# Filler matmuls of a hybrid encoder's two attentions, listed by hand for three zones

## The chip, the cores and the metric

The kernel runs on one core of a Trainium2 chip. The core has TensorE (PE, matrix products into PSUM), VectorE (DVE), ScalarE (ACT), GpSimd (POOL) and SyncE (SP, which here only issues DMAs). The metric is the device time of one execution in microseconds; the time before is the median of three executions, 1702.64 us (1701.64 to 1703.32).

## The reference

Two layers of an encoder on one sequence of 512 tokens with 1024 features. Per layer:

```python
h = rms_norm(x, attn_norm_g[l])
c_q, c_kv, k_rope, gq, gk, gv, pool_in, gate_logits = split_columns(h @ w_in[l], IN_SIZES)
o_mla  = mla_branch(...)   # 8 heads; q = rms_norm(c_q) @ w_uq, k and v from rms_norm(c_kv) @ w_ukv,
                           # q and k of 96 (64 + 32 rotary) normalised per head
o_gqa  = gqa_branch(...)   # 8 heads of 64 on 2 key/value heads, normalised, rotary
o_pool = pool_branch(...)  # centred means over 2/4/8/16 tokens minus the token, mixed per group
gates  = sigmoid(gate_logits)                      # 3 x 1024 per token
merged = gates[0] * (o_mla @ w_branch_mla) + gates[1] * (o_gqa @ w_branch_gqa) \
       + gates[2] * (o_pool @ w_branch_pool)
x = x + merged @ w_out[l]
x = x + GatedMLP(rms_norm(x, ffn_norm_g[l]))       # width 2816, depthwise conv of 3
```

## The kernel before

Activations lie feature-major in SBUF (128 features by 512 tokens). For precision every operand of a product is split into a high and a low part, and each product is three matmuls (`mm3`: high by high, high by low, low by high). Weights come by DMA in a fixed order of pieces (`w_dma`, three raw buffers ahead), and ScalarE and GpSimd split each piece (`w_split`: `wh`, then `wl`).

The program is written out by hand-made scheduling at build time. `Clock` holds a planned time; `chain` queues the follow-up steps of a result on VectorE, ScalarE and GpSimd at the planned time at which they can run; `need` advances the planned time until a key is recorded by `done`; `has` asks whether a key has been recorded by now and says no for one that is not there. The order of the instructions on each engine comes from this plan; on the chip semaphores keep the data right.

A layer does, in order: latents and the pool branch; keys and values of the grouped attention; its queries; then three steps with two attentions in them:

- the first attention (`gqa`), then the second (`mla`), eight heads each. `attention` walks a list of steps with places (`PLAN`): transposes of the queries and keys (`t_q`, `t_k`, PSUM bank `mi`), four score products with a row maximum on VectorE (`s_max`, bank `S`, result `nm`), the maxima as a row (`m_row`, bank `mi`, written into `qa`), and for each of four key blocks the transposed scores (`probs`, two banks `ST`), exponential `pe`, high part `ph`, low part `pl`, and the value products (`av_hi` with `ph`, `av_lo` with `pl`, bank `AV`). `o_out` copies a head's output, takes the reciprocal of the sums and splits the product (`oh`, `ol`).
- between these steps PE is given other matmuls, the filler. Its units are three matmuls (six for the latent units): a gate block `g` has 8 units and a branch block `b` has 4, both 512 columns wide; `q` (4 units) and `n` (2) make half of the latent attention's queries and keys, `v` (2) half of its values. All use the two PSUM banks `acc`. `Filler.step` runs one unit, `upto` runs up to a count, `finish` the rest.
- before, the filler of the first attention is made of the pool branch's gates and blocks, both `q` and both `n`; that of the second of the grouped branch's gates and blocks and both `v`; the latent branch's gates and blocks run after it. `_order` lists them: a gate block, then the branch block before it, with the latent units put in at places given by `EXTRA`.

Ahead of the first attention the filler runs for 13 units and then until the keys and queries are recorded as ready; ahead of the second for 17 units and then in this loop:

```python
fb.upto(PRE_B)
while not ck.has(("mq", l, 0)) and fb.step():
    pass
attention("mla", fb, "om", omla)
```

`q_norm(g)`, the last of the queries' steps, ends with `done("mq", l, g)`; `t_q` of the second attention asks for `("mq", l, h // 4)`.

Of the kernel before, what the change touches and what calls it, by code (L numbers as in the profile page):

```python
# [18 lines left out]
P = 128  # L19
T = 512  # L20
# [9 lines left out]
NSLOT = 53  # L30
RAW = 3
EXTRA = (("q", 2, (2, 5)), ("n", 2, (6, 7)), ("v", 1, (0, 3)))
# [25 lines left out]
def _order(br):  # L58


    r = []
    for m in range(KC + 1):
        r += [(k, pos.index(m)) for k, b, pos in EXTRA if b == br and m in pos]
        if m < KC:
            r.append(("g", m))
        if m > 0:
            r.append(("b", m - 1))
    return r
# [6 lines left out]
def _widths():  # L75

    r = [384] * KC + [T] * 8 + [288] * KC + [T] * 4 + [T] + [T] * 4
    for br in (2, 1, 0):
        for k, _ in _order(br):
            r += WIDTHS[k]  # L80
    return r + [T] * (2 * KC) + [T] * (4 * FC) + [T] * (2 * FC)
# [162 lines left out]
def trunk(ctx: ExitStack, tc: tile.TileContext, x, w, prm, gb, cst, out):  # L244
# [244 lines left out]
    def layer(l, sq, xsrc):  # L489
# [289 lines left out]
        def gates(br, okey, odst, mode):  # L779
            hold = {}  # L780

            def gate(m):
                acc = ps("acc")
                yield from feat_major(acc, G1)
                t = hold[m] = slot("gt")

                def logits():
                    V.tensor_tensor(t[:, :T], acc, nrm["rbc"][:, :T], ALU.mult)
                    free("acc")

                chain(([("rbc", G1)], logits), lambda: A.activation(t[:, :T], t[:, :T], AF.Tanh, scale=0.5))

            def branch(m):
                acc = ps("acc")
                wh, wl = wnext()
                for kc in range(4):
                    if kc:
                        yield
                    need((okey, l, kc))
                    ws = slice(kc * P, kc * P + P)  # L800
                    oh, ol = odst[kc]
                    mm3(acc, wh[:, ws], wl[:, ws], oh[:, :T], ol[:, :T], kc == 0, kc == 3)
                t = hold.pop(m)

                def product():
                    dst = XM[:, m, :] if mode == "first" else t[:, :T]
                    V.scalar_tensor_tensor(dst, t[:, :T], 1.0, acc, ALU.add, ALU.mult)
                    free("acc")

                def add():  # L810
                    (V if mode == "last" else G).tensor_tensor(XM[:, m, :], XM[:, m, :], t[:, :T], ALU.add)

                def fin():
                    SY.dma_start(XM[:, m, :], xsrc[m])
                    done("mrg", l, m)

                if mode == "first":
                    chain(product)
                elif mode == "add":
                    chain(product, add)  # L820
                else:
                    mh, ml = slot("mgh", F32R), slot("mgl", F32R)
                    merged[m] = (mh, ml)
                    chain(product, add, *split(mh[:, :T], ml[:, :T], XM[:, m, :]), fin)

            extra = None
            for k, m in _order(br):
# [3 lines left out]
                work = branch(m) if k == "b" else gate(m)  # L831
                more = True
                while more:
                    if extra:
                        if next(extra, END) is END:
                            extra = None
                        yield
                    more = next(work, END) is not END
                    yield
# [4 lines left out]
        krr = small("krr", [P, 4, 32], bufs=1)  # L844

        def make_q(g):
# [53 lines left out]
        def make_n(g):  # L900
# [9 lines left out]
            if g == 0:  # L910
                return
            kj_ = small("kj", [P, 4, 32], bufs=1)
            kss = small("kss", [P, 4], bufs=1)

            def sums():
                V.tensor_reduce(kss, kj_, AX.X, ALU.add)
                for i in range(2):
                    V.tensor_tensor(ss[:, 1, i], ss[:, 1, i], bc(kss.unsqueeze(2), [P, 4, 4]), ALU.add)
                V.tensor_scalar(ss[:, 1], ss[:, 1], 1.0 / 96, EPS, ALU.mult, ALU.add)
# [4 lines left out]
            chain(*rope_steps(krr, krt, tabm[:, 256:384].rearrange("p (b f) -> p b f", b=4),  # L924
                              tabm[:, 384:512].rearrange("p (b f) -> p b f", b=4), [P, 4, 32], 16, V),
# [581 lines left out]
```

## Time and profile before

| | |
|---|---|
| median of three executions | 1702.64 us |
| the profiled execution | 1701.64 us |
| its span, first to last instruction | 1699.4 us |
| mean granted TensorE clock | 0.994 |
| PE busy | 1655.1 us, 97% |
| DVE, ACT, POOL busy | 938.3, 782.6, 972.3 us |
| first attention with its filler, layer 0 | about 113 to 245 us |
| second attention with its filler, layer 0 | about 245 to 373 us |
| gates and blocks behind it, layer 0 | about 373 to 441 us |

A row of the views below names line, engine, operation, output and inputs; in a window's row each engine has its busy time and count, and PEclk is the granted share of the TensorE clock. PE's busy times are modelled for pipelined matmuls, so that the starts of two neighbours say more than the length of one.

### The profile page before, as it was taken

Reading aid. Unit: us, or ns where it says so; the run is one execution under the profiler, and the core shown is the slowest. Engines: PE = TensorE matmul, PEld = TensorE weight load, DVE = VectorE, ACT = ScalarE, POOL = GpSimd, SP = SyncE. Lnnn points to the kernel's source line nnn. Section 1 sums busy time; section 2 is a strip of 40 time slices with the busy share of each in tenths; the row PEclk is TensorE's granted clock in tenths of the full one; section 3 lists DMA queues with packets and bytes.
Section 4 is the critical chain, followed back from the end, with each engine's and each line's share of the span. In section 5 each row is a group of like instructions: output and inputs, shape, how many; then the busy total and the mean of one; then the engine's idle time right before and its main releaser. Section 6 shows DMA issues by size and latency. Waiting matters only on the chain.

```text
span 1699.4 us, 20370 instructions
## 1 busy us (share of the span) xinstructions
PE 1655.1 (97%) x7360; PEld 1335.7 (79%) x7360; DVE 938.3 (55%) x1502; ACT 782.6 (46%) x1375; POOL 972.3 (57%) x771
## 2 busy tenths in 40 slices
PE   8889999999999999999999899999999999999999
PEld 7767767778888888888888677777788888888887
DVE  6765976643356666630156759766433666666100
ACT  5356655653344444433234576556534444444221
POOL 4455565764566566655545565666645665666543
PEclk9999999999999999999999999999999999999999
DMA  5221112113423332333333211111233232232331
GB/s 176 85 72 44 56 48 62 38 62 112 124 87 89 98 100 87 100 106 116 100 101 95 70 44 47 61 49 38 75 118 118 87 100 92 94 94 93 111 118 56
DMA packets 44596, 145.40 MB, mean 86 GB/s; under 512 B 5072, under 2 KB 6352, under 8 KB 44496
## 3 DMA queue, kind: packets, MB, share of 16 engines
q1 hardware_dynamic: 44352, 144.10, 27.0%
q8 instruction: 58, 0.95, 0.2%
q14 instruction: 42, 0.34, 0.1%
q10 hardware_dynamic: 144, 0.01, 0.0%
HBM read 139.90 MB, written 4.19 MB: 85 GB/s over the span
## 4 chain that ended last, share of the span: by engine, by line
PE 87%; DVE 8%; issue 2%; ACT 1%; POOL 1%; DMA 0%; SPq 0%; POOLq 0%; DVEq 0%; ACTq 0%
PE ps_acc L341 40%; PE ps_ST L341 23%; PE ps_AV L341 20%; PE ps_S L341 2%; DVE gqr L216 1%; PE ps_mi L345 1%; DVE yt L216 1%; DVE nm L224 1%; POOL wl L216 1%; PE ps_mi L341 1%; DVE MQ L216 1%; DVE yt L220 0%; DVE win L216 0%; DVE y L220 0%; DVE y L228 0%
## 5 line engine op out<-in xcount | busy, mean ns | idle before, releaser
L216 POOL TENSOR_TENSOR wl<-raw,wh 128x512 fp32r<-128x512 f32 (+1 forms) x514 | 678.5, 1330 | 493.4 <-ACT wh L209 432.1
L209 ACT ACTIVATE wh<-raw 128x512 fp32r<-128x512 f32 (+3 forms) x522 | 313.8, 608 | 194.2 <-PE ps_ST L341 70.8
L220 DVE SCALAR_TENSOR_TENSOR a<-u,prm,a 128x512 f32<-128x512 f32 x176 | 239.6, 1362 | 79.2 <-ACT a L209 74.0
L341 PE MATMUL ps_acc<-HH,wh 128*128 128x512 f32 x624 | 247.1, 396 | 2.2 <-DVE XM L220 2.2
L341 PE MATMUL ps_acc<-HH,wl 128*128 128x512 f32 x624 | 246.7, 395 | 1.2 <-POOL wl L216 1.2
L341 PE MATMUL ps_acc<-HL,wh 128*128 128x512 f32 x624 | 246.2, 395 | 0.0
L216 POOL TENSOR_TENSOR pl<-pe,ph 128x512 fp32r<-128x512 f32 x105 | 138.9, 1325 | 110.4 <-ACT ph L209 70.4
L341 PEld LDWEIGHTS ps_acc<-HH,wh 128*128 128x128 f32 x624 | 117.5, 188 | 30.8 <-ACT mns L209 2.1
L341 PEld LDWEIGHTS ps_acc<-HH,wl 128*128 128x128 f32 x624 | 117.3, 188 | 30.0 <-POOL wl L216 2.5
L341 PEld LDWEIGHTS ps_acc<-HL,wh 128*128 128x128 f32 x624 | 117.5, 188 | 26.8
L209 ACT ACTIVATE pe<-ps_ST 128x512 f32<-128x512 f32 x128 | 76.3, 596 | 101.8 <-PE ps_ST L341 100.4
L224 DVE TENSOR_REDUCE nm<-ps_S 128x1 fp32r<-128x512 f32 x128 | 87.8, 686 | 57.3 <-PE ps_S L341 57.0
L216 POOL TENSOR_TENSOR al<-a,ah 128x512 fp32r<-128x512 f32 x44 | 58.1, 1320 | 84.8 <-ACT ah L209 56.5
L341 PE MATMUL ps_AV<-HH,wh 128*128 128x512 f32 x256 | 101.3, 396 | 0.0
L341 PE MATMUL ps_AV<-HH,wl 128*128 128x512 f32 x256 | 101.2, 395 | 0.0
L341 PE MATMUL ps_AV<-HL,wh 128*128 128x512 f32 x256 | 101.1, 395 | 0.0
L341 PE MATMUL ps_ST<-HH,wh 128*128 128x512 f32 x240 | 95.0, 396 | 0.0
L341 PE MATMUL ps_ST<-HH,wl 128*128 128x512 f32 x240 | 94.8, 395 | 0.0
L341 PE MATMUL ps_ST<-HL,wh 128*128 128x512 f32 x240 | 94.8, 395 | 0.0
L209 ACT ACTIVATE a<-u,prm 128x512 f32<-128x512 f32 x88 | 71.8, 816 | 32.4 <-DVE u L216 32.4
L209 ACT ACTIVATE ah<-a 128x512 fp32r<-128x512 f32 x44 | 27.8, 632 | 116.2 <-DVE u L240 110.8
L209 ACT ACTIVATE a<-a 128x512 f32<-128x512 f32 x44 | 27.8, 633 | 113.5 <-DVE u L240 113.5
(332 smaller groups left out, 3563.3 us busy)
## 6 DMA issues: line engine op xcount, KB each, us to landing
raw<-w SPq DMA_DIRECT2D x229, 512.0 KB, 3.5
raw<-w SPq DMA_DIRECT2D x13, 384.0 KB, 3.0
XM<-x SPq DMA_DIRECT2D x16, 256.0 KB, 3.8
raw<-w SPq DMA_DIRECT2D x6, 448.0 KB, 3.4
xsp<-XM SPq DMA_DIRECT2D x8, 256.0 KB, 2.0
XM<-xsp SPq DMA_DIRECT2D x8, 256.0 KB, 3.2
out<-XM SPq DMA_DIRECT2D x8, 256.0 KB, 2.5
raw<-w SPq DMA_DIRECT2D x4, 432.0 KB, 3.2
```

Of the source, the lines that this page charges most:

```text
L209: return self.eng.activation(out, in_, func, **k)
L216: return self.eng.tensor_tensor(out, *a)
L220: return self.eng.scalar_tensor_tensor(out, *a)
L224: return self.eng.tensor_reduce(out, in_, *a, **k)
L341: PE.matmul(o, lhsT=lhsT, rhs=rhs, start=start, stop=stop)
L345: PE.transpose(o, src, ident)
```

## The change

The filler is no longer made per branch but listed for three zones: beside the first attention, beside the second, and behind it. Zone 0 loses the second `q` and `n` and gains three gate blocks of the grouped branch (126 units for 108). Zone 1 has the rest of that branch, both `v`, the second `q` and `n`, and three gate blocks of the latent branch (106 for 100). Zone 2 is what is left (72 for 96). The results of gates that run ahead are held in SBUF slots, of which there is one more. The normalisation of the latent queries and keys is made per half, with its own sums, reciprocal roots and ready keys, and the key's rotary part with the first `n`. The weight pieces are packed in the new order. The loop ahead of the second attention asks for another key.

```diff
-NSLOT = 53
+NSLOT = 54
-EXTRA = (("q", 2, (2, 5)), ("n", 2, (6, 7)), ("v", 1, (0, 3)))
+ZONES = (
+    "g20 g21 b20 q0 g22 b21 g23 b22 g24 b23 n0 g25 b24 g26 b25 g27 b26 g10 b27 g11 g12",
+    "v0 g13 g14 q1 b10 g15 n1 b11 g16 b12 v1 g17 b13 g00 b14 g01 b15 g02 b16 b17",
+    "g03 g04 g05 g06 g07 b00 b01 b02 b03 b04 b05 b06 b07")
...
+def _zone(z):
+    return [(k[0], int(k[1]) if len(k) == 3 else None, int(k[-1])) for k in ZONES[z].split()]
...
-            if g == 1:
-                chain(([("ssq", l, i, b) for i in range(2) for b in range(4)],
-                       lambda: V.tensor_scalar(ss[:, 0], ss[:, 0], 1.0 / 96, EPS, ALU.mult, ALU.add)),
-                      *rsqrt_steps(ss[:, 0].rearrange("p g b c -> p (g b c)"), 32, ("ssmq", l)),
-                      *[z for i in range(2) for z in q_norm(i)])
+            chain(([("ssq", l, g, b) for b in range(4)],
+                   lambda: V.tensor_scalar(ss[:, 0, g], ss[:, 0, g], 1.0 / 96, EPS, ALU.mult, ALU.add)),
+                  *rsqrt_steps(ss[:, 0, g].rearrange("p b c -> p (b c)"), 16, ("ssmq", l, g)), *q_norm(g))
...
-            chain(lambda: V.tensor_tensor(kj_, krt, krt, ALU.mult), ([("ssn", l, i, p) for i in range(2) for p in range(2)], sums),
-                  *rsqrt_steps(ss[:, 1].rearrange("p g b c -> p (g b c)"), 32, ("ssm", l)),
-                  *[z for i in range(2) for z in k_norm(i)])
+            chain(([("ssn", l, g, 0), ("ssn", l, g, 1), ("kss", l)], sums),
+                  *rsqrt_steps(ss[:, 1, g].rearrange("p b c -> p (b c)"), 16, ("ssm", l, g)), *k_norm(g))
...
-        fa = Filler(gates(2, "op", opool, "first"), units(2))
+        def filler(z):
+            return Filler(work(z), sum(UNITS[k] for k, _, _ in _zone(z)))
+        fa = filler(0)
...
-        fb = Filler(gates(1, "og", ogqa, "add"), units(1))
+        fb = filler(1)
         fb.upto(PRE_B)
-        while not ck.has(("mq", l, 0)) and fb.step():
+        while not ck.has(("mq", l, 0, 3)) and fb.step():
             pass
         attention("mla", fb, "om", omla)
-        Filler(gates(0, "om", omla, "last"), units(0)).finish()
+        filler(2).finish()
```

More of the change, by code (lines that the diff above doesn't have):

```diff
@@ L77, in _widths @@
     r = [384] * KC + [T] * 8 + [288] * KC + [T] * 4 + [T] + [T] * 4
-    for br in (2, 1, 0):
-        for k, _ in _order(br):
+    for z in range(3):
+        for k, _, _ in _zone(z):
             r += WIDTHS[k]
@@ L777, in layer @@
         merged = {}
[L779 to L824, printed above, removed]
@@ new lines, in layer, with gate, logits @@
+        ogqa, omla, hold = {}, {}, {}
+        branches = {2: ("op", opool, "first"), 1: ("og", ogqa, "add"), 0: ("om", omla, "last")}
+        def gate(br, m):
+            acc = ps("acc")
+            yield from feat_major(acc, G1)
+            t = hold[br, m] = slot("gt")
+            def logits():
+                V.tensor_tensor(t[:, :T], acc, nrm["rbc"][:, :T], ALU.mult)
+                free("acc")
+            chain(([("rbc", G1)], logits), lambda: A.activation(t[:, :T], t[:, :T], AF.Tanh, scale=0.5))
@@ L826, in gates, with work @@
+        def work(z):
             extra = None
-            for k, m in _order(br):
+            for k, br, m in _zone(z):
                 if k in mla_make:
@@ L830, in gates @@
                     continue
-                work = branch(m) if k == "b" else gate(m)
+                step = branch(br, m) if k == "b" else gate(br, m)
                 more = True
@@ L837, in gates @@
                         yield
-                    more = next(work, END) is not END
+                    more = next(step, END) is not END
                     yield
```

64 lines of the change are left out of this document (40 added, 24 removed).

## The prediction

> **What bounds the kernel now.** I read the page first, then the stretches, the waits of TensorE, and the timeline around the second attention.
>
> ```profile
> span 1699.4 us, 20370 instructions
> ...
> PE 1655.1 (97%) x7360; PEld 1335.7 (79%) x7360; DVE 938.3 (55%) x1502; ACT 782.6 (46%) x1375; POOL 972.3 (57%) x771
> ...
> PE 87%; DVE 8%; issue 2%; ACT 1%; POOL 1%; DMA 0%; SPq 0%; POOLq 0%; DVEq 0%; ACTq 0%
> ```
>
> TensorE (PE) is busy for 97% of the span and is 87% of the chain that ended last. So a change of order can win only PE's idle time, and it loses wherever it makes PE wait. The stretches of layer 0 show where that idle time is (first attention 113 to 245 us, second 245 to 373, the rest of the third gates 373 to 441):
>
> ```profile
> core 0: us, PE busy (x) PEld busy (x) DVE busy (x) ACT busy (x) POOL busy (x), PEclk, DMA share, GB/s
> 113.00:245.00 132.00, 121.60 (x538) 94.72 (x539) 102.28 (x164) 87.06 (x157) 71.78 (x58) 0.97 0.15 47
> 245.00:373.00 128.00, 127.86 (x597) 101.78 (x596) 77.38 (x114) 71.85 (x128) 83.49 (x75) 1.00 0.17 53
> 373.00:441.00 68.00, 68.00 (x294) 54.98 (x293) 25.45 (x37) 24.70 (x42) 32.73 (x27) 1.00 0.39 116
> ```
>
> The first attention leaves PE idle for 10.4 us, the second for 0.14 us, the last stretch for none. The second attention is thus already covered by the gate and branch matmuls mixed into it. What PE waits for in the first one:
>
> ```profile
> PE ps_S L341 <- DVE nm L224: 4.3, 4, 2.7
> PE ps_mi L345 <- DVE gk L216: 3.7, 1, 3.7
> PE ps_acc L341 <- ACT mqs L209: 1.2, 2, 0.9
> ...
> PE ps_acc L341 <- DVE vml L216: 0.9, 1, 0.9
> ```
>
> **The change, part by part.** The diff moves work, and it also changes one key. Before, the loop ahead of the second attention takes single units of filler until `("mq", l, 0)` is recorded; now it asks for `("mq", l, 0, 3)`. The only writer, at the end of `q_norm`, still records `("mq", l, g)`. The four-part key is never written, so the loop ends only when `fb.step()` has nothing left: all 106 units of the second zone go ahead of the attention, and the attention gets none. The order of the changed kernel's instructions on TensorE bears this out. After the last branch matmul come transposes, scores and values alone, up to the last head:
>
> ```
> L338 Matmult ps_acc_3052<-oh_2407,wl_3015 128x512
> L342 Matmult ps_mi_3071<-C,MQ_84 96x128 x4
> L342 Matmult ps_mi_3082<-C,MK_86 96x128 x4
> L338 Matmult ps_S_3093<-kh_3087,qa_3077 128x512
> L342 Matmult ps_mi_3096<-C,MQ_84 96x128 x4
> L338 Matmult ps_S_3103<-kh_3087,qa_3077 128x512
> ```
>
> So the main cost is a second attention without cover, twice. TensorE runs the same matmuls in all.
>
> *PE's work in the bare attention.* Matmuls of 512 columns start every 0.233 us, and a row of four transposes takes 0.35:
>
> ```profile
> 269.38 0.60 PE L345 MATMUL ps_mi<-C,MK 128*96 128x128 f32 x4
> 269.73 0.47 PE L341 MATMUL ps_ST<-qa,kl 96*128 96x512 f32 x1
> ...
> 360.79 0.39 PE L341 MATMUL ps_ST<-qa,kh 100*128 100x512 f32 x1
> 361.02 0.40 PE L341 MATMUL ps_AV<-ph,vmh 128*128 128x512 f32 x1
> ...
> 361.22 0.60 ACT L209 ACTIVATE pe<-ps_ST 128x512 f32<-128x512 f32 x1 [1.24 <-PE ps_ST L341]
> ...
> 361.85 0.63 ACT L209 ACTIVATE ph<-pe 128x512 fp32r<-128x512 f32 x1
> ...
> 362.56 1.29 POOL L216 TENSOR_TENSOR pl<-pe,ph 128x512 fp32r<-128x512 f32 x1 [0.90 <-ACT ph L209]
> ```
>
> A head has four score maxima (S), four key blocks of three probability matmuls (P) and three value matmuls (two with ph, one with pl), which is 28 x 0.233, and 0.70 for its transposes and 0.06 for the row of maxima (M): 7.28 us. Eight heads: 58.3 us.
>
> *The waits.* A block's chain starts with its third P: 0.43 to the exponential, 0.63, 0.71 and 1.29 to the end of pl, 0.1 to PE: 3.16 us. In the built order the pl matmul of block k stands ahead of P of block k+2, with only block k+1 between. Two blocks hence take at least 3.16 + 3 x 0.233 = 3.86, and a head 7.7. The side engines add their queues, with these durations:
>
> ```profile
> L224 DVE TENSOR_REDUCE nm<-ps_S 128x1 fp32r<-128x512 f32 x32 | 22.0, 686 | 13.5 <-PE ps_S L341 13.4
> L236 DVE RECIPROCAL osum<-osum 128x128 f32<-128x128 f32 x16 | 14.6, 930 | 0.0
> L220 DVE SCALAR_TENSOR_TENSOR qb<-ps_mi,gcol,qa 96x512 fp32r<-96x512 f32 x8 | 5.7, 716 | 5.6 <-ACT qa L209 5.6
> ...
> L216 DVE TENSOR_TENSOR qa<-ps_mi,C 4x512 fp32r<-4x512 f32 x8 | 5.5, 684 | 1.7 <-PE ps_mi L341 1.5
> L216 DVE TENSOR_TENSOR kl<-ps_mi,kh 96x512 fp32r<-96x512 f32 x8 | 5.5, 682 | 0.2
> ...
> L232 DVE CAST ph<-pe 128x512 fp32r<-128x512 f32 x8 | 4.8, 602 | 12.5 <-ACT pe L209 10.2 <-POOL XM L216 2.2
> ...
> 358.25 1.01 DVE L216 TENSOR_TENSOR oraw<-oraw,osum 128x512 f32<-128x512 f32 x1
> ...
> L209 ACT ACTIVATE qa<-ps_mi,gcol 96x512 fp32r<-96x512 f32 x8 | 5.4, 674 | 5.5 <-PE ps_mi L345 5.5
> L209 ACT ACTIVATE kh<-ps_mi 96x512 fp32r<-96x512 f32 x7 | 4.1, 590 | 0.0
> L209 ACT ACTIVATE oh<-oraw 128x512 fp32r<-128x512 f32 x4 | 2.5, 629 | 6.2 <-DVE oraw L216 6.2
> L216 POOL TENSOR_TENSOR ol<-oraw,oh 128x512 fp32r<-128x512 f32 x3 | 3.9, 1293 | 1.3 <-ACT oh L209 1.3
> L240 POOL MEMSET kh<- 4x512 f32 x8 | 4.5, 563 | 0.5
> ```
>
> I walk one head, zero at its first P, each engine in its built order. A plain head: P to 0.7, transposes of the next keys, kh to 2.0, kl to 2.7; transposes of the next queries after it (one bank, mi); S0 at 2.1 and its nm to 3.45; S1 at 3.7; pl of block 0 ready at 3.45; block 2 ends near 4.9; qb and nm1 put S2 at 5.6; block 3 follows pl of block 1 (6.3); S3 at 7.2, its nm to 8.3, M at 8.4, three value matmuls, next P at 9.1. A head beside which a pair's output is normalised has four reciprocals between the maxima: from nm0 at 2.97, VectorE runs 4 x 0.69 + 4 x 0.93 + 0.72 + 0.68 without a gap to 10.3, and the next head's third P needs its last result (the row of maxima): 9.8. In the head after it, oh stands ahead of the exponential (0.7 later) and ol with the memset ahead of pl (pl of block 0 ends near 5.0): 9.5. Ahead of head 0 the first transposes, qb, kl, four S and nm, and M follow each other with nothing beside: 9.1. The last head runs to its last pl: 9.5. Sum: 9.1 + 2 x 9.1 + 3 x 9.8 + 2 x 9.5 + 9.5 = 85.2 us, of which PE works 58.3. **Waits: 26.9 us per layer.** Lowest: 9.1 + 8 x 7.7 - 58.3 = 12.4. Highest: 36, if the side engines' operations collide (an oraw product took 1.01 us, a cast of ph took 0.60) and each head takes 1.1 more. I take the walk.
>
> *The clock.* After an idle stretch PE runs at half clock:
>
> ```profile
> 50.08:53.49 3.41, 1.39 (x6) 0.76 (x5) 3.41 (x8) 0.61 (x2) 0.98 (x1) 1.00 0.00 0
> 53.50:56.91 3.41, 1.13 (x3) 0.54 (x3) 3.38 (x16) 0.63 (x1) 0.00 (x0) 0.50 0.00 0
> ...
> 190.03:193.44 3.41, 3.41 (x9) 2.64 (x9) 3.38 (x7) 1.75 (x3) 0.28 (x1) 0.50 0.29 119
> 900.00:903.41 3.41, 1.95 (x13) 1.50 (x12) 3.41 (x5) 2.97 (x7) 1.82 (x3) 1.00 0.00 0
> ...
> 190.58 0.63 PE L341 MATMUL ps_acc<-opl,wh 128*128 128x512 f32 x1
> 191.00 0.63 PE L341 MATMUL ps_acc<-oph,wl 128*128 128x512 f32 x1
> ```
>
> At 190 us, after the wait of 2.7 us, matmuls start every 0.42 to 0.43 us for 3.41 us: some 8 of them, 0.195 later each, 1.6 us lost. The window with 1.39 us busy was followed by half clock, that with 1.95 was not. The bare attention's start holds 1.7 us of PE work in 9.1, so half clock follows it: **+1.6 per layer** (0 to 4).
>
> *First attention.* Its filler grows from 108 units to 126, and half of the latent queries' and keys' normalisation leaves its VectorE, busy for 102.28 of 132 us. The gk wait stays (it stands ahead of the moved work), as does the one on vml. Of the remaining 10.4 - 3.7 - 0.9 = 5.8 us, and the 1.6 of half clock behind the longest wait, I take two thirds: **-5.0** (0 to -7.4).
>
> *Ahead of the second attention.* q and n units now stand between branch units that hold the other of the two acc banks, so each waits for the last one's evacuation: **+1.0**, about what the same units cost in the first attention (ACT mqs 1.2); 0 to 4. The 42 further small VectorE operations are mostly the second copies of the reciprocal root's steps:
>
> ```profile
> L220 DVE SCALAR_TENSOR_TENSOR yt<-yt,y x36: 152/190/1190, 30.3 to 1334.5; 128x8 f32<-128x8 f32 x18, 128x32 f32<-128x32 f32 x12, 128x40 f32<-128x40 f32 x6
> ```
>
> At a median of 0.19 us the 21 of a layer are 4 us. They are hidden by VectorE's idle 50 us of 128; uncovered they would cost those 4 us. Weights are only reordered: same DMAs on SP's queue, same halves; ScalarE and POOL keep up, as with this mix in 373 to 441 us. The second attention's own idle 0.14 goes: **-0.1**. The last zone shrinks by 24 units that ran without idle time and run without it elsewhere: 0. The slot more only takes memory.
>
> Sum per layer: 26.9 + 1.6 - 5.0 + 1.0 - 0.1 = 24.4; two layers 48.8. The profiled execution took 1701.64 us (span 1699.4), 1.0 below the median of 1702.64, so against that median 1751.
>
> **Rivals.**
> *The clock stays low.* The walk's thinnest 3.41 us in a head with reciprocals holds some 1.6 us of matmul starts, 2.2 busy as the windows count, not far above 1.95. If every other window ran at half clock, PE's 7.28 us per head would take 3.1 more; with half of it on the path, 8 x 1.5 = 12 per layer: 1775. Against it: the one window of 1.95. The Trainium skill, "TensorE: Matmul & The Clock Gate", section "HAM oscillation — how this bites in real kernels", asks only for gaps under about 3.4 us, by which no wait between heads would lower the clock; the trace disagrees, as 2.7 us did. Its section on the second failure mode says that frequent small gaps make the clock swing; that would be this rival.
> *The side engines do better.* Without weight splits and gates, ACT and POOL are free when a block arrives, and a head takes 8.4, midway between the chain's 7.7 and the plain head's 9.1: waits 9.1 + 67.2 - 58.3 = 18.0, sum per layer 15.5, 1734. Against it: the order of VectorE's queue between the maxima is fixed.
> *Not slower: the change does what its words say.* If the loop ahead of the second attention stopped early, as before, the attention would keep its cover and only the first one's gain would stay: 2 x -5.0, 1693. It decides from some 35 units (three matmuls, 0.70 us each) left beside the attention, which cover those 24.4 us. Against it: the built order, where none is left.
>
> **How the numbers follow.** Forecast 1751: 0.60; clock stays low 0.16; side engines do better 0.19; not slower 0.05, most of it below. The forecast's neighbours reach down to the lowest waits with the full gain (2 x (12.4 + 1.6 - 7.4 + 1.0 - 0.1) = +15, 1718) and up to highest waits with half clock recurring (2 x (36 + 4 - 3 + 1) = +76, 1779, with the clock's 24 more 1803). The range 1725 to 1788 leaves out about 2 in 10. 0.2% (3.4 us) is about what a measurement can tell. Slower 0.95, within it 0.01, faster 0.04.
>
> **What would show it.** In the changed profile: in each layer some 85 us of second attention with PE busy near 70% and only scores, values and transposes on it; PE's waits led by pl from POOL, nm and the row qa from VectorE, and kl; half clock at the start of each; under 7 us idle in the first attention; no idle time in the last zone. A head period of 8.4 or less, filler between the heads, or half clock in most windows would make it wrong.

## The result, and the profile after

The changed kernel takes 1780.99 us (median of four executions, 1777.66 to 1783.73) against 1702.98 us for the kernel before in the same series: 1.0455 times as long, 95% interval 1.0429 to 1.0481. That is 78 us more, where the forecast had 48.8. The profiled execution has a span of 1781.9 us.

From here on a line number of the changed kernel is three lower than the same line's before (L341 is L338, L216 is L213). The page after, with the rows that the prediction began with:

```profile
span 1781.9 us, 20502 instructions
...
PE 1688.0 (95%) x7360; PEld 1343.0 (75%) x7360; DVE 961.2 (54%) x1544; ACT 782.3 (44%) x1366; POOL 985.1 (55%) x782
...
PE 80%; DVE 14%; ACT 2%; issue 2%; POOL 2%; DMA 1%; SPq 0%; POOLq 0%; DVEq 0%; ACTq 0%
```

TensorE runs the same 7360 matmuls. Its share of the chain of work that ended last falls from 87% to 80%, and VectorE's rises from 8% to 14%, POOL's from 1% to 2%. The stretches of layer 0 after: the first attention, the filler that now stands alone, the bare second attention, the last zone.

```profile
core 0: us, PE busy (x) PEld busy (x) DVE busy (x) ACT busy (x) POOL busy (x), PEclk, DMA share, GB/s
121.40:255.20 133.80, 125.08 (x543) 98.08 (x544) 88.08 (x136) 77.68 (x137) 71.99 (x56) 0.97 0.17 53
...
255.00:341.90 86.90, 79.50 (x350) 63.33 (x349) 39.95 (x72) 29.44 (x55) 46.36 (x44) 0.98 0.26 82
341.90:430.00 88.10, 71.84 (x297) 46.02 (x296) 55.35 (x81) 52.62 (x89) 50.59 (x45) 0.94 0.00 1
430.00:480.00 50.00, 50.00 (x216) 40.37 (x217) 23.57 (x30) 18.20 (x31) 22.91 (x18) 1.00 0.35 112
```

The bare attention is there as the built order had it: 88 us, no weights moving (DMA share 0.00), TensorE 16 us idle by the row (busy times are modelled longer than the pitch of the starts, by which it works 58.3 us). But the stretch ahead of it, which is nothing but filler, idles 7.4 us too. TensorE's waits over the whole span:

```profile
PE ps_mi L338 <- DVE nm L221: 23.0, 20, 3.6
PE ps_S L338 <- DVE nm L221: 9.3, 10, 2.5
PE ps_acc L338 <- DVE gt L213: 9.0, 2, 4.5
PE ps_AV L338 <- POOL pl L213: 7.8, 14, 0.9
```

Before, the largest of these sums was `PE ps_S L341 <- DVE nm L224`, 8.4 us in all, and the gate's evacuation `gt` was not among the first six. Each `gt` wait of 4.5 us is one per layer.

The lengths below run from the first transposes of an attention to the last value matmul, worked from TensorE's starts (layer 0 / layer 1, us). The zones' PE work is that of the prediction's 0.70 us for a gate unit: zone 0 has 24 gate units more and the six units of the second `q` and `n` less, +11.2; zone 1 +5.6; zone 2 -16.8.

| stretch | before | after | less the moved work: waits | forecast |
|---|---|---|---|---|
| first attention | 121.6 / 121.7 | 133.8 / 135.4 | +1.0 / +2.5 | -5.0 |
| between, and second attention | 130.1 / 130.1 | 174.8 / 176.1 | +39.1 / +40.4 | +29.4 |
| of it, the bare attention's waits (length less 58.3) | | 29.8 / 30.2 | 29.8 / 30.2 | 28.5 |
| last zone | 68.4 / 68.2 | 50.4 / 50.3 | -1.2 / -1.1 | 0 |
| a layer | 320.1 / 319.9 | 359.0 / 361.8 | +38.9 / +41.8 | +24.4 |

The bare attention came within 1.3 to 1.7 us of its forecast. Of the 14.5 us that layer 0 has more than forecast, 6.0 are in the first attention and 8.4 in the filler ahead of the second. The experiments had to say why.

### The profile page after: what moved, and what is told of

Read it like the earlier page. It is cut to its first block, busy times and chain, and to the rows that moved or that the text cites. A ratio compares the mean times of both kernels' runs of the same rounds, so it can differ in the third digit from the quotient of the medians.

```text
span 1781.9 us, 20502 instructions
## 1 busy us (share of the span) xinstructions
PE 1688.0 (95%) x7360; PEld 1343.0 (75%) x7360; DVE 961.2 (54%) x1544; ACT 782.3 (44%) x1366; POOL 985.1 (55%) x782
## 3 DMA queue, kind: packets, MB, share of 16 engines
q1 hardware_dynamic: 44352, 144.10, 24.4%
## 4 chain that ended last, share of the span: by engine, by line
PE 80%; DVE 14%; ACT 2%; issue 2%; POOL 2%; DMA 1%; SPq 0%; POOLq 0%; DVEq 0%; ACTq 0%
PE ps_acc L338 35%; PE ps_ST L338 21%; PE ps_AV L338 19%; PE ps_S L338 2%; DVE nm L221 2%; DVE XM L213 1%; PE ps_mi L342 1%; DVE gqr L213 1%; DVE osum L233 1%; DVE yt L213 1%; PE ps_mi L338 1%; POOL pl L213 1%; DVE gt L217 1%; DVE mgl L213 1%; DVE yt L217 1%
## 5 line engine op out<-in xcount | busy, mean ns | idle before, releaser
L213 POOL TENSOR_TENSOR wl<-raw,wh 128x512 fp32r<-128x512 f32 (+2 forms) x514 | 679.3, 1330 | 552.5 <-ACT wh L206 479.4
L338 PE MATMUL ps_acc<-HH,wh 128*128 128x512 f32 x624 | 248.4, 398 | 0.5 <-ACT mqs L206 0.5
L338 PE MATMUL ps_acc<-HH,wl 128*128 128x512 f32 x624 | 247.6, 397 | 0.5 <-POOL wl L213 0.5
L338 PE MATMUL ps_acc<-HL,wh 128*128 128x512 f32 x624 | 247.5, 397 | 0.0
L213 POOL TENSOR_TENSOR pl<-pe,ph 128x512 fp32r<-128x512 f32 x116 | 151.4, 1306 | 112.6 <-ACT ph L206 77.3
L338 PEld LDWEIGHTS ps_acc<-HH,wh 128*128 128x128 f32 x624 | 118.5, 190 | 29.1 <-ACT mqs L206 1.4
L338 PEld LDWEIGHTS ps_acc<-HH,wl 128*128 128x128 f32 x624 | 118.1, 189 | 28.8 <-POOL wl L213 0.9
L338 PEld LDWEIGHTS ps_acc<-HL,wh 128*128 128x128 f32 x624 | 118.4, 190 | 27.4
L221 DVE TENSOR_REDUCE nm<-ps_S 128x1 fp32r<-128x512 f32 x128 | 87.2, 682 | 58.6 <-PE ps_S L338 58.0
L213 POOL TENSOR_TENSOR al<-a,ah 128x512 fp32r<-128x512 f32 x44 | 58.1, 1321 | 84.8 <-ACT ah L206 72.7
L338 PE MATMUL ps_AV<-HH,wh 128*128 128x512 f32 x256 | 101.3, 396 | 0.0
L338 PE MATMUL ps_AV<-HH,wl 128*128 128x512 f32 x256 | 101.1, 395 | 0.0
L338 PE MATMUL ps_AV<-HL,wh 128*128 128x512 f32 x256 | 101.1, 395 | 0.0
L338 PE MATMUL ps_ST<-HH,wh 128*128 128x512 f32 x240 | 95.0, 396 | 0.0
L338 PE MATMUL ps_ST<-HH,wl 128*128 128x512 f32 x240 | 94.8, 395 | 0.0
L338 PE MATMUL ps_ST<-HL,wh 128*128 128x512 f32 x240 | 94.8, 395 | 0.0
L213 DVE TENSOR_TENSOR gt<-ps_acc,rbc 128x512 f32<-128x512 f32 x48 | 33.1, 690 | 108.3 <-PE ps_acc L338 107.2
```

Source lines behind the costliest of these rows:

```text
L213: return self.eng.tensor_tensor(out, *a)
L221: return self.eng.tensor_reduce(out, in_, *a, **k)
L338: PE.matmul(o, lhsT=lhsT, rhs=rhs, start=start, stop=stop)
```

## The experiments

**The key alone, and the key undone.** In the kernel before, one edit:

```diff
-        while not ck.has(("mq", l, 0)) and fb.step():
+        while not ck.has(("mq", l, 0, 3)) and fb.step():
```

> The kernel before, with nothing changed but the key that the loop ahead of the second attention asks for. Theory (the second attention without cover makes most of the loss): the same 30 us of waits per layer as in the changed kernel's bare attention (88.1 us of which PE works 58.3), nothing from the lists: 1703 + 60 = 1763 (1755 to 1770). Rival (the moved gates, queries and keys make the loss): 1703 to 1712.

Measured: 1763.36 against 1700.82 us, ratio 1.0368 (1.0351 to 1.0385). Its filler stretch and its bare attention in layer 0:

```profile
242.20:314.40 72.20, 70.49 (x314) 56.91 (x313) 19.94 (x33) 23.20 (x42) 45.03 (x43) 1.00 0.29 93
314.40:402.80 88.40, 72.35 (x299) 46.31 (x297) 55.19 (x81) 52.64 (x89) 50.34 (x45) 0.94 0.00 1
```

The bare attention is the same 88 us with the old lists and the old normalisation, so the key alone makes it. The filler ahead of it, without latent queries and keys in it, idles 1.7 us, not 7.4.

The other way round, the changed kernel with the old key:

```diff
-        while not ck.has(("mq", l, 0, 3)) and fb.step():
+        while not ck.has(("mq", l, 0)) and fb.step():
```

> The changed kernel with the old key, all else as changed, so that the zones stand as they are listed and the second attention has its filler. Theory: the cover returns and the 30 us per layer go, and so does most of the 11 us of waits in the stretch ahead of it; what the first attention lost (1 to 2.5 us per layer) stays, less 1.2 us won in the last zone: 1706 (1699 to 1715). Rival (the moved work makes the loss): 1760 or more.

Measured: 1720.09 against 1700.82 us, 1.0119 (1.0103 to 1.0135). The key costs some 62 us, as forecast; but what is left of the change, which the prediction had as a gain (-5.0 in the first attention), costs 19. The expected 1706 was missed. The two parts, 62.5 and 19.3, make 81.8, near the 78.0 of the whole change.

**Which part of the rest?** The key undone, and the old lists put back by hand, so that only the normalisation per half is left of the change:

```diff
 ZONES = (
-    "g20 g21 b20 q0 g22 b21 g23 b22 g24 b23 n0 g25 b24 g26 b25 g27 b26 g10 b27 g11 g12",
-    "v0 g13 g14 q1 b10 g15 n1 b11 g16 b12 v1 g17 b13 g00 b14 g01 b15 g02 b16 b17",
-    "g03 g04 g05 g06 g07 b00 b01 b02 b03 b04 b05 b06 b07")
+    "g20 g21 b20 q0 g22 b21 g23 b22 g24 b23 q1 g25 b24 n0 g26 b25 n1 g27 b26 b27",
+    "v0 g10 g11 b10 g12 b11 v1 g13 b12 g14 b13 g15 b14 g16 b15 g17 b16 b17",
+    "g00 g01 b00 g02 b01 g03 b02 g04 b03 g05 b04 g06 b05 g07 b06 b07")
```

> The changed kernel with the old key and with the lists of before (both halves of queries and keys beside the first attention, gates by branch): of the change only the normalisation per half is left, 42 small VectorE operations more. Theory (these operations are held by GpSimd's splits, up to 1.2 us each, ahead of the row maxima that PE waits for): 3 to 8 us slower than before, 1706 to 1711. Rival (at 0.19 us each they are hidden, as the prediction had it): 1703.

Measured: 1721.99, 1.0128 (1.0112 to 1.0145). That is well above the 1706 to 1711 expected: all of the 19 us, and a little more, is in the normalisation per half, not in the lists. The first attention lasts 132.6 us in layer 0 and 133.7 in layer 1, instead of 121.6 and 121.7; no other stretch of the table above differs by more than 0.3 us.

The changed kernel's trace shows what such operations can meet, in its filler stretch (POOL's and VectorE's rows of the timeline, and at the end the matmul of TensorE that waited):

```profile
280.65 1.31 POOL L213 TENSOR_TENSOR XM<-XM,gt 128x512 f32<-128x512 f32 x1
280.76 1.24 DVE L213 TENSOR_TENSOR yt<-y,ssm 128x16 f32<-128x16 f32 x1
...
281.91 2.54 POOL L213 TENSOR_TENSOR wl<-raw,wh 128x512 fp32r<-128x512 f32 x2
282.03 1.22 DVE L217 SCALAR_TENSOR_TENSOR yt<-yt,y 128x16 f32<-128x16 f32 x1
283.28 1.21 DVE L217 SCALAR_TENSOR_TENSOR y<-yt,y 128x16 f32<-128x16 f32 x1
284.52 0.18 DVE L213 TENSOR_TENSOR yt<-y,ssm 128x16 f32<-128x16 f32 x1
...
285.78 1.83 DVE L213 TENSOR_TENSOR MQ<-MQ,ssm 128x768 f32<-128x768 f32 x2
...
288.39 0.69 DVE L213 TENSOR_TENSOR gt<-ps_acc,rbc 128x512 f32<-128x512 f32 x1
...
289.23 0.47 PE L338 MATMUL ps_acc<-oh,wh 128*128 128x512 f32 x1 [4.49 <-DVE gt L213]
```

The second half's root chain and products stand in VectorE's queue ahead of `gt`, which evacuates a gate and frees one of the two `acc` banks; TensorE waits 4.49 us for it. Three root steps of 16 elements take 1.2 us each, and each ends within 0.1 us of the end of a POOL operation (`x2` is two back to back); from 284.52, when POOL is done, the same step takes 0.18. So, in these rows, a small operation with two inputs is held until POOL's operation is over. The row over all of them, of before and of after, shows how far a median is from that:

```profile
L216 DVE TENSOR_TENSOR yt<-y,ssm x12: 191/432/1184, 183.3 to 1063.5; 128x32 f32<-128x32 f32 x12
```

```profile
L213 DVE TENSOR_TENSOR yt<-y,ssm x24: 164/177/1239, 132.6 to 1182.9; 128x16 f32<-128x16 f32 x24
```

(Three numbers with slashes are the shortest, the median and the longest in ns.) The Trainium skill, "SBUF — State Buffer", section "Who interferes with whom", says that a VectorE instruction with two SBUF inputs contends with a GpSimd instruction that reads SBUF, and calls the ports that the two engines share an exclusive lock. The trace agrees: 0.18 us alone, about 1.2 beside POOL.

The other 2.9 of the 7.4 idle us of this stretch are waits for `vml` (1.8) and `mqs` (1.1). Behind the long wait TensorE runs one window at half clock:

```profile
289.69:293.10 3.41, 3.41 (x13) 2.56 (x12) 1.30 (x3) 2.19 (x6) 1.27 (x1) 0.50 0.01 2
```

With the 1.6 us that the prediction worked out for such a window, that is 9.0, near the 9.3 us that layer 0 loses there (39.1 less the bare attention's 29.8).

**How much do these operations cost?** First, fewer in the changed kernel: one Newton step for the 16-wide roots instead of three.

```diff
+        first = [] if n == 16 else [*newton(y), *newton(y)]
         return [lambda: V.tensor_scalar(y.bitcast(I32), a.bitcast(I32), -0.5, RSQRT_BITS, ALU.mult, ALU.add),
-                *newton(y), *newton(y), *newton(a), lambda: done(*key)]
+                *first, *newton(a), lambda: done(*key)]
```

> The changed kernel with one Newton step in place of three in the reciprocal roots of the latent queries and keys (two of three are left out, so the roots are less exact): 48 small VectorE operations less, which together hold about 22 us of VectorE by the changed kernel's trace. Theory (held by GpSimd, they delay what PE waits for): 8 to 14 us faster than the changed kernel, 1767 to 1773. Rival (hidden): 1779 to 1781.

Measured: 1769.8, 1.0407 (1.0389 to 1.0424): 11 us less than the changed kernel for 48 operations less, 0.23 us each (9 us, if each is taken against the kernel before in its own series: 69.0 and 78.0). All of it is in the first attentions, which last 129.1 and 128.6 us instead of 133.8 and 135.4. The filler stretch is as long as before this edit (87.0 us) and TensorE's wait for `gt` even longer, 4.7 us: the chain is six steps shorter, but in this build two more of its products (`MQ`) stand ahead of `gt`. So fewer root steps did not shorten that wait; where `gt` stands in VectorE's queue decides it. Then more of them in the kernel before: five steps for its 32-wide roots.

```diff
-                *newton(y), *newton(y), *newton(a), lambda: done(*key)]
+                *newton(y), *newton(y), *(newton(y) + newton(y) if n == 32 else []), *newton(a), lambda: done(*key)]
```

> The kernel before with five Newton steps in place of three in the four reciprocal roots of the latent queries and keys: 24 small VectorE operations more, nothing else (the result hardly moves). Theory (their number is what the per-half normalisation costs, 23 us for 44 more in the kernel with the old lists, 0.5 us each): 8 to 14 us slower than before. Rival (hidden; what costs is the new place of the long multiplications): 0 to 2 us.

Measured: 1711.63 against 1701.61, 1.0058 (1.0038 to 1.0079): 10 us for 24 operations, 0.42 us each. So further work on VectorE in the first attention is not hidden, though VectorE is busy for only 77% of that stretch (93.94 of 121.60 us) and 55% of the span.

**The lists without the second set of roots.** From the kernel with the key undone: one root chain per half for queries and keys together, so that there are as many small operations as before.

```diff
-            chain(([("ssq", l, g, b) for b in range(4)],
-                   lambda: V.tensor_scalar(ss[:, 0, g], ss[:, 0, g], 1.0 / 96, EPS, ALU.mult, ALU.add)),
-                  *rsqrt_steps(ss[:, 0, g].rearrange("p b c -> p (b c)"), 16, ("ssmq", l, g)), *q_norm(g))
...
-            chain(([("ssn", l, g, 0), ("ssn", l, g, 1), ("kss", l)], sums),
-                  *rsqrt_steps(ss[:, 1, g].rearrange("p b c -> p (b c)"), 16, ("ssm", l, g)), *k_norm(g))
+            chain(([("ssq", l, g, b) for b in range(4)] + [("ssn", l, g, 0), ("ssn", l, g, 1), ("kss", l)], sums),
+                  *rsqrt_steps(ss[:, g].rearrange("p k b c -> p (k b c)"), 32, ("ssm", l, g)), *q_norm(g), *k_norm(g))
...
```

> The changed kernel with the old key and one root chain per half for queries and keys together, so that there are as many small VectorE operations as before, with the new lists and the normalisation per half. Theory (the number of small operations costs): the 19 us of the kernel with the old key alone fall to 0 to 6, 1701 to 1707. Rival (the places cost): 1715 to 1722.

Measured: 1702.46 against 1701.61, 1.0004 (0.999 to 1.0019). The moved gates and halves cost nothing and win nothing that can be measured. In layer 0 the first attention lasts 125.9 us with 11.2 us more work, so its waits do shrink, by 6.9 us; the second lasts 130.9 instead of 117.0 with 5.6 us more work, which gives 8.3 back (in layer 1, 6.7 won and 6.0 given back).

**Number, or place?** The old lists with one Newton step per half: 40 small operations in all, 44 before.

```diff
-                *newton(y), *newton(y), *newton(a), lambda: done(*key)]
+                *([] if n == 16 else newton(y) + newton(y)), *newton(a), lambda: done(*key)]
```

> The kernel with the old lists and the normalisation per half, with one Newton step in place of three (two are left out, so the roots are less exact): fewer small operations than before (40 for 44 in the trace). Theory: the 21 us of that kernel fall to 0 to 5, 1701 to 1706. Rival (the places cost): 1713 or more.

Measured: 1719.98, 1.0104 (1.0081 to 1.0127): only 2 us less than with all three steps, where 1701 to 1706 was expected. A price per small operation does not explain this. And the kernel with joint roots, but with the two chains of a half separate again, both begun where the joint one begins:

```diff
-            chain(([("ssq", l, g, b) for b in range(4)] + [("ssn", l, g, 0), ("ssn", l, g, 1), ("kss", l)], sums),
-                  *rsqrt_steps(ss[:, g].rearrange("p k b c -> p (k b c)"), 32, ("ssm", l, g)), *q_norm(g), *k_norm(g))
+            chain(([("ssq", l, g, b) for b in range(4)] + [("ssn", l, g, 0), ("ssn", l, g, 1), ("kss", l)],
+                   lambda: V.tensor_scalar(ss[:, 0, g], ss[:, 0, g], 1.0 / 96, EPS, ALU.mult, ALU.add)),
+                  *rsqrt_steps(ss[:, 0, g].rearrange("p b c -> p (b c)"), 16, ("ssmq", l, g)), *q_norm(g),
+                  sums, *rsqrt_steps(ss[:, 1, g].rearrange("p b c -> p (b c)"), 16, ("ssm", l, g)), *k_norm(g))
```

> As the kernel with joint roots (new lists, old key), but with a root chain of its own for the queries and one for the keys of each half, both begun where the joint one is begun: the number of small VectorE operations of the changed kernel at the places of the joint one. Theory A (the number costs): 1714 to 1722, near the 1720 of the kernel with the old key alone. Theory B (the place costs, above all the query chain that falls into the first heads of the first attention): 1703 to 1709.

Measured: 1718.11 against 1702.72, 1.0095 (1.008 to 1.011). Here the place was kept, and the second set of roots costs 15 us (15.4 against the kernel before, to which the joint roots were equal). About 10 of them are in the first attentions (131.1 and 131.3 us instead of 125.9 and 126.2), about 4 in the second ones.

What the lengths of these kernels' first attentions follow, within the same lists, is VectorE's busy time there. The rows of that stretch in layer 0, one fence a kernel; first the old lists: the kernel before, five Newton steps, one step per half, three steps per half.

```profile
120.50:242.10 121.60, 113.97 (x507) 88.86 (x508) 93.94 (x147) 80.34 (x145) 66.70 (x53) 0.99 0.15 48
```

```profile
119.70:246.30 126.60, 115.23 (x507) 88.86 (x508) 100.27 (x159) 80.54 (x145) 66.86 (x53) 0.99 0.14 46
```

```profile
121.10:252.70 131.60, 118.16 (x508) 90.95 (x509) 102.27 (x151) 78.81 (x142) 65.25 (x50) 0.96 0.14 45
```

```profile
120.40:253.00 132.60, 116.37 (x507) 89.91 (x508) 107.85 (x173) 78.76 (x142) 67.38 (x52) 0.97 0.14 44
```

Then the new lists: joint roots, the two chains of a half begun late, and the changed kernel with one step per half (the changed kernel's own row, 88.08 in 133.80, stands above).

```profile
120.60:246.50 125.90, 122.19 (x543) 96.09 (x544) 81.71 (x124) 78.09 (x138) 72.28 (x56) 1.00 0.17 56
```

```profile
120.70:251.80 131.10, 123.12 (x543) 95.78 (x544) 88.28 (x135) 78.42 (x138) 72.84 (x56) 1.00 0.17 54
```

```profile
123.80:252.90 129.10, 124.17 (x544) 97.31 (x545) 85.38 (x127) 77.28 (x136) 69.72 (x53) 0.99 0.17 55
```

With the same TensorE work in each group, each us more of VectorE's time (fifth column) makes the stretch longer by 0.8 (five steps: 6.3 and 5.0; three steps per half: 13.9 and 11.0; late chains: 6.6 and 5.2) to 1.2 (one step per half: 8.3 and 10.0; the changed kernel against joint roots: 6.4 and 7.9). The changed kernel with one step per half gives more, 1.7 (2.7 us less than the changed kernel and 4.7 shorter). The granted clock does not order them, but it is part of these prices: half clock lasts one window of 3.41 us where the row has 0.99, two at 0.97, three at 0.96 and none at 1.00. If each window costs at most 1.7 us, between 0.7 and 1.1 per us of VectorE's time remain. Between the two groups the price does not hold: the changed kernel's VectorE is busy 5.9 us less there than before's, and its waits are still 1.0 us longer.

VectorE's time also offers a reading of why one step per half did not help in the old lists: VectorE is busy 8.3 us longer than before although it runs no more root steps. The rows of VectorE's groups in the first attention, before and with the old lists and one step per half:

```profile
L216 DVE TENSOR_TENSOR pl<-pe,ph 128x512 fp32r<-128x512 f32 x6 | 4.6, 768 | 0.1
...
L216 DVE TENSOR_TENSOR MQ<-MQ,ssm 128x768 f32<-128x768 f32 x4 | 3.7, 949 | 0.0
```

```profile
L213 DVE TENSOR_TENSOR pl<-pe,ph 128x512 fp32r<-128x512 f32 x9 | 6.9, 772 | 0.1
L213 DVE TENSOR_TENSOR MQ<-MQ,ssm 128x768 f32<-128x768 f32 x4 | 5.9, 1498 | 0.1
...
L229 DVE CAST qa<-ps_mi 64x512 fp32r<-64x512 f32 x2 | 1.4, 688 | 1.0 <-ACT qa L206 0.8 <-PE ps_mi L342 0.2
```

The planner gave VectorE three more splits `pl` (+2.3) and two casts `qa` (+1.4), and the products of the normalisation, with two inputs like the root steps, take longer (`MQ` by `ssm`: four take 5.9 instead of 3.7).

The reading by VectorE's time came from the traces after the runs, so it was put to a test of its own: the kernel before with few, long, single-input operations in the same place, four reductions of 128x1536 per layer that nothing reads.

```diff
+        def unread(g):
+            d = small("unr", [P, 16], bufs=1)
+            V.tensor_reduce(d, MQ[g].rearrange("p b h f -> p (b h) f"), AX.X, ALU.max)
...
                       *rsqrt_steps(ss[:, 0].rearrange("p g b c -> p (g b c)"), 32, ("ssmq", l)),
+                      *[lambda i=i: unread(i) for i in range(2)],
...
                   *rsqrt_steps(ss[:, 1].rearrange("p g b c -> p (g b c)"), 32, ("ssm", l)),
+                  *[([("ssq", l, i, b) for b in range(4)], lambda i=i: unread(i)) for i in range(2)],
```

> The kernel before, with four further VectorE reductions of 128x1536 per layer whose results nothing reads (two of the queries behind each of the two reciprocal roots, so as not to change any other work): eight long operations in the run, some 1.65 us each by the row maxima (0.686 us for 512 elements per partition), 6.5 us of VectorE per layer, all in the first attention. Theory: the first attention lasts longer by 0.8 to 1.2 us for each us of VectorE time added in it, whatever the operations are (24 small ones in the run with five Newton steps added 6.3 us of VectorE time and 5.0 us to the first attention of layer 0): 5 to 8 per layer, 1711 to 1718. Rival: what costs is a number of short dependent operations, 0.42 us each in that run: eight operations give 3.4, 1705. Rival: long operations with one input are not held behind GpSimd's and hide in VectorE's idle time: 1702 to 1703.

Measured: 1715.07 against 1702.98, 1.0072 (1.0054 to 1.009), and in the trace the stretch and the reductions:

```profile
119.60:246.70 127.10, 115.53 (x507) 90.46 (x508) 102.10 (x148) 80.40 (x145) 69.36 (x55) 0.97 0.14 46
```

```profile
L224 DVE TENSOR_REDUCE unr<-MQ x8: 1734/1744/1748, 188.4 to 1076.1; 128x16 f32<-128x1536 f32 x8
```

Eight long operations cost 12 us, where eight short ones at 0.42 would cost 3. VectorE is busy 8.2 us longer (7.0 of it the reductions) and the first attention lasts 5.5 us longer, 0.7 per us. The row's clock is 0.97, two windows at half clock against one before, so up to 1.7 of the 5.5 us are the clock's. What the first attention does not hide is thus VectorE's time, whatever the number of its operations.

**The half clock at the start of the bare attention.** The changed kernel with 22 further matmuls per layer that nothing reads, in the waits ahead of its head 0:

```diff
+            def warm(n):
+                d = ps("acc")
+                for _ in range(n):
+                    mm(d, HH[:, 0, 0:P], HH[:, 0, :], True, True)
...
+                if h == 0:
+                    warm(7)
...
+                if h == 0:
+                    warm(3)
...
+                if not gqa and h == 0 and b > 0:
+                    warm(4)
```

> The changed kernel with 22 matmuls per layer added whose result nobody reads, put in the waits ahead of head 0 of the bare attention, 5.1 us of PE work in some 7 us of waiting. Theory (the windows at half clock stretch head 0 to 11.1 us where the next takes 8.7): the clock stays full there, head 0 takes 8.7 to 9.3, 3 to 5 us faster than the changed kernel in all, 1776 to 1778. Rival (the clock costs nothing, since PE waits anyway): head 0 stays at 11 us, 1781 or a little more.

Measured: 1778.05, 1.0446 (1.0427 to 1.0464), 3 us less than the changed kernel, but only 1.6 against the kernel before in each series (76.4 and 78.0), which is within the two intervals. The row over head 0's start shows full clock, as it was meant to:

```profile
341.00:352.00 11.00, 9.66 (x44) 6.15 (x42) 6.13 (x9) 1.96 (x3) 2.28 (x3) 1.00 0.00 0
```

Head 0 went from 11.13 (layer 1: 10.90) to 9.92 us in both layers, not to the 8.7 to 9.3 expected, so half clock costs that head about 1 us. Of the bare attentions as wholes (88.8 and 87.2, against 88.1 and 88.5) only the second shows it: in the first, a window at half clock fell into the last head, which took 12.3 us instead of 10.7.

```profile
419.70:423.10 3.40, 1.64 (x7) 0.70 (x6) 1.05 (x1) 2.91 (x6) 2.83 (x3) 0.99 0.00 0
423.10:426.50 3.40, 3.40 (x9) 2.55 (x9) 0.00 (x0) 1.23 (x2) 1.27 (x2) 0.50 0.00 0
```

The same happened in layer 1 of the kernel with the key alone (12.0 us, behind a window with TensorE busy for 1.69 us).

**Could the lists win with joint roots?** Two more lists on that kernel: all halves beside the first attention, and the second halves in the short stretch between the attentions.

```diff
-    "g20 g21 b20 q0 g22 b21 g23 b22 g24 b23 n0 g25 b24 g26 b25 g27 b26 g10 b27 g11 g12",
-    "v0 g13 g14 q1 b10 g15 n1 b11 g16 b12 v1 g17 b13 g00 b14 g01 b15 g02 b16 b17",
+    "g20 g21 b20 q0 g22 b21 g23 b22 n0 g24 b23 q1 g25 b24 n1 g26 b25 g27 b26 g10 b27 g11 g12",
+    "v0 g13 g14 b10 g15 b11 g16 b12 v1 g17 b13 g00 b14 g01 b15 g02 b16 b17",
```

> As the kernel with joint roots, but with both halves of queries and keys beside the first attention, and the three gates more there as in the change: of the listed moves only the gates are left. Theory (VectorE's norm work is what makes an attention wait, the gates fill for nothing): the second attention falls back to 117 us and what its work needs, the first one keeps its 10 us of waits or some less: 1698 to 1704. Rival (more filler alone covers the first attention's waits): 1688 to 1695.

Measured: 1703.62 against 1702.72, 1.001 (0.9999 to 1.0022): no gain.

```diff
-    "v0 g13 g14 q1 b10 g15 n1 b11 g16 b12 v1 g17 b13 g00 b14 g01 b15 g02 b16 b17",
+    "v0 g13 q1 g14 n1 b10 g15 b11 g16 b12 v1 g17 b13 g00 b14 g01 b15 g02 b16 b17",
...
-PRE_B = 17
+PRE_B = 36
```

> As the kernel with joint roots, but the second halves of queries and keys come first in the second zone and 36 units instead of 17 run ahead of the second attention, so that their norms run on VectorE while neither attention asks for row maxima. Theory (norms beside an attention's row maxima are what costs): the first attention keeps the 7 us per layer that the joint kernel won, the second loses most of the 7 that it lost: 1688 to 1695, faster than before. Rival (the stretch between has its own waits on the two acc banks): 1700 to 1704.

Measured: 1722.9, 1.0121 (1.0105 to 1.0137), 28 us above the highest time that the theory allowed and 19 above the rival's. TensorE's waits from the stretch between the attentions to the end of the second, layer 0:

```profile
PE ps_mi L342 <- DVE qb L217: 2.5, 1, 2.5
PE ps_acc L338 <- DVE vml L213: 2.3, 2, 1.4
PE ps_mi L338 <- DVE nm L221: 1.9, 1, 1.9
PE ps_AV L338 <- POOL pl L213: 1.9, 3, 0.6
```

The 19 units more ahead of the attention are missing at its end: the waits for `pl` fall into its last head. The stretch between has waits of its own (0.9 us for `vml`, 1.2 for `mqs`), and the attention's start waits 2.5 us for `qb`. No version was faster than the kernel before.

## Why the prediction was right, and where its sizes were off

**The missing key: right.** The key that nothing records sends all of zone 1 ahead of the attention. Undoing it took 61 us off (1780.99 to 1720.09), doing it alone cost 62.5.

**The walk of the bare attention: right in its sum, 85.2 + 1.6 forecast, 88.1 and 88.5 measured.** The rows that bound its first heads (a head runs from one first P to the next):

```profile
344.08 0.64 PE L342 MATMUL ps_mi<-C,MK 128*96 128x128 f32 x4 [1.55 <-DVE qb L217]
...
351.17 0.27 PE L338 MATMUL ps_mi<-idr,nm 128*4 128x128 f32 x1 [0.78 <-DVE nm L221]
351.23 0.74 PE L338 MATMUL ps_ST<-qa,kl 96*128 96x512 f32 x1
...
362.36 0.40 PE L338 MATMUL ps_ST<-qa,kl 96*128 96x512 f32 x1
...
371.06 0.40 PE L338 MATMUL ps_ST<-qa,kl 96*128 96x512 f32 x1
```

The start took 9.30 (9.1 walked); head 0, at half clock, 11.13 (9.1); then 8.70, 9.42, 10.18, 9.41, 10.17, 9.06 (walked 9.1, 9.8, 9.5, 9.8, 9.5, 9.8), and the last 10.75 (9.5). So the heads with reciprocals were shorter than walked and the heads after them longer: the row of maxima holds the third P of the head after, and part of the delay is counted there. A pair of such heads took 19.6 to 19.8 where the walk has 19.3, so the sum is better than its parts. One figure of the walk does not come out: the durations listed for VectorE in such a head add up to 7.88, which from 2.97 ends at 10.85 and not at 10.3; its own figures would have made that head 10.4 and the sum 86.9. The waits are among those named, as far as the view of waits puts them down, but nm leads (6.3 + 1.9), not pl (3.9):

```profile
PE ps_mi L338 <- DVE nm L221: 6.3, 8, 0.8
PE ps_AV L338 <- POOL pl L213: 3.9, 7, 0.9
PE ps_S L338 <- DVE nm L221: 1.9, 3, 0.8
PE ps_mi L342 <- DVE qb L217: 1.6, 1, 1.6
```

The row `qa` holds back the weight load of the third P, not a matmul, and stands in the weight loads' waits: `PEld ps_ST L338 <- DVE qa L213: 1.7, 3, 0.6`, at the three heads that follow one with reciprocals.

**The clock: the place was right, its length too short.** Half clock came at the start of the bare attention, for three windows (10.2 us in both layers) instead of one. The window before, the first and the third of them, and the one after:

```profile
344.30:347.71 3.41, 2.01 (x10) 0.93 (x8) 1.73 (x3) 1.27 (x2) 0.97 (x2) 1.00 0.00 0
347.71:351.12 3.41, 1.59 (x2) 0.58 (x2) 2.28 (x4) 0.00 (x0) 0.00 (x0) 0.50 0.00 0
...
354.54:357.95 3.41, 3.41 (x11) 2.45 (x10) 2.10 (x4) 1.92 (x4) 2.35 (x2) 0.50 0.00 0
357.95:361.36 3.41, 2.82 (x12) 1.76 (x10) 1.87 (x4) 1.99 (x4) 1.14 (x1) 1.00 0.00 0
```

Much of it fell into waits, so that head 0 lost about 1 us to it by the run with the further matmuls, near the forecast 1.6.

**"First attention -5.0": wrong, +1.0 and +2.5.** The step that failed is "They are hidden by VectorE's idle 50 us of 128", said of the 42 further small operations. It took VectorE's idle time over a stretch of 128 us for cover. That stretch is the second attention before; about half of the operations run beside the first (the first step at 132.6 us), whose row left VectorE idle for 30 of 132 us. And idle time is no cover: of VectorE's 27.7 idle us in the first attention before (121.60 less 93.94), 15.3 stand ahead of a maximum `nm` that waits for its scores, and what is queued ahead of that maximum delays TensorE. It also priced the operations at a median of 0.19 us, where those beside POOL take about 1.2. Of the prediction's signs, "under 7 us idle in the first attention" failed with it: the row has 8.7 (133.80 less 125.08). With as many operations as before (joint roots) the term comes out at -6.9 and -6.7: the mechanism behind the -5.0 was there, and the second set of roots took it back.

**"Ahead of the second attention +1.0": wrong, +9 to +10.** The prediction priced the wait for the last unit's evacuation by ScalarE's `mqs` (1.2 in the first attention), and that wait came as priced (1.1). It left out the gate's evacuation `gt`, on VectorE behind the root chain and the products of the second half's normalisation (4.49 us, the timeline above), `vml` (1.8, of which 0.9 was there before), and the half clock behind the long wait (some 1.6).

**The rest.** The last zone was 1.2 us shorter than its lost work, forecast 0; why is open. In layer 0 the two wrong terms make 6.0 and 8.4 of the 14.5 us missed.

**The rivals.** *The clock stays low* fell: from 358 us to the end of that attention the granted clock is 1.00, and the row's mean of 0.94 is the three windows at the start (10.2 us at half are 5.1 of 88.1, 6%). The single windows in the last head, in two bare attentions of other runs, show that it was not far off. The Trainium skill, "TensorE: Matmul & The Clock Gate", section "A second HAM failure mode: psum-queue depth-cycling", has small frequent gaps that make the clock swing. These gaps of about 0.8 us did not do so here. *The side engines do better* fell: no head was under 8.7. *Not slower* fell with the built order, and would have fallen without it: with the attention covered (key undone) the kernel is 19 us slower all the same, for the second set of roots.

## What to carry to other kernels

A key that is asked for and never recorded changes no result here, only the order; read the built order at each wait of such a planner, and price an attention without cover by walking one head (here 30 us of waits per layer). Before calling further work on a side engine hidden, ask what stands behind it in that engine's queue: in a stretch where VectorE gives TensorE its next operand, each us more or less on VectorE changed the stretch by 0.7 to 1.7 us, half clock included, though VectorE was busy for 77% of that stretch and 55% of the span. Batch chains of small dependent operations (one root over 32 columns instead of two over 16), and price two-input operations beside POOL by their longest rows, not by the median.

## What was not expected of the hardware

- A VectorE operation with two inputs from SBUF, of 16 elements, took 0.18 us alone and about 1.2 beside a POOL operation, ending with it. The reductions with one input, 1536 elements, took 1734 to 1748 ns, all eight alike, in the same stretch with POOL busy for 69 of 127 us. The Trainium skill, "SBUF — State Buffer", section "Who interferes with whom", says that a reduction never contends on this chip. This row agrees.
- Half clock followed a window in which the rows show TensorE busy 2.01 of 3.41 us, while before one with 1.95 was not followed by it. So busy time by these rows gives no clean bound. One stop can cost three windows of half clock: the first of them, with TensorE waiting, is no busier (1.59); why the third came, behind one with 3.37, is not shown.
